# Two-network kernel: convolution taps without GpSimd, a re-ordered background preparation, and a new order of the first down tiles

## The chip, the cores and the metric

One core of a Trainium2 chip runs the whole program. The metric is device microseconds of one execution, the median of three runs. PE is TensorE, DVE is VectorE, ACT is ScalarE, POOL is GpSimd and SP is SyncE, whose queue issues the program's DMAs.

## The reference

A latent stream `x` and a context stream of 256 tokens each, 1024 wide, pass through two networks of two layers. Each layer is a half feed forward, a mixer, and another half feed forward. The three parts that the change touches compute:

```python
def _swiglu(h, wg, wu, wd):                       # each feed forward, D_FF = 2816
    return (jax.nn.silu(h @ wg) * (h @ wu)) @ wd

def _conv_module(h, w1, b1, wdw, bdw, lng, lnb, w2, b2):   # mixer of layer 0, first network
    a, gt = jnp.split(h @ w1 + b1, 2, axis=-1)
    u = a * jax.nn.sigmoid(gt)
    u = depthwise_conv(u, wdw, width=31) + bdw
    u = jax.nn.silu(_layernorm(u, lng, lnb))
    return u @ w2 + b2

def s5_discretise(lam_re, lam_im, b_re, b_im, log_step):   # mixer of layer 1, second network
    ...                                           # depends on weights alone
```

The S5 mixer's tables (powers of the diagonal, their products with B and C, a Toeplitz kernel) depend on weights alone, so they can be made at any time before the mixer.

## The kernel before, in words

Activations are kept transposed, features on partitions, in 8 tiles of 128. A matrix product in 32-bit precision is made of three matmuls (high x high, low x high, high x low) by `gemm`; `pump` splits each weight piece of 128x1024 into its high part (ACT, line 180) and low part (line 185, on DVE, or on GpSimd for every second piece when `cvm` is 2). Five pieces are held ready at most (`NBUF`), and `release` frees them and asks for the next.

**Feed forward** (`ffn`). The stages are named f100, f102, f110, f112 for the first network (layer, then 0 or 2 for the first or second half) and f200 to f212 for the second. The 22 hidden tiles are made in groups of 6, 8 and 8 (`FGROUPS`): for each hidden tile the products `gu` (gate and up), then `glu`: silu on ACT (`sg`, line 775), product on DVE (line 777), high part `Hh` on ACT (line 779), low part `Hl` on DVE (line 780). After a group come its 8 down tiles `pd`, each a sum over the group's hidden tiles (`down`), added to the stream by `scalar_tensor_tensor` or `tensor_add`. f112 and f212 have one stream of 256 columns, the others two (512 columns).

**Convolution** (`conv`, lines 947 to 1146). For each feature tile m the product `pw1` (48 matmuls) gives `u`. The 31 taps are shared out: 8 are scaled on ACT (line 998) and added up on GpSimd (line 999, tile `a`), 5 are matmuls with diagonal weights on PE (`ptap`), the other 18 run on DVE (line 1004) in two accumulators `v` and `b`; the sums meet in lines 1007, 1021 and 1022. The last tile has 7 on GpSimd and 12 on PE. `cvm` is 2 here. Then a layer norm (means by matmul, `pmean`) and `pw2`.

**S5 preparation** (`s5_pre`, lines 1853 to 2107) is a generator that runs as a `Task` beside f100, f102 and f110, with a period of 820 ns of the planner's PE time. A bare `yield` gives one period, `yield n` at least n ns. It makes 8 blocks d; in each, two directions r. For each r, GpSimd makes 6 wide products (`A8`, `B8`, lines 2015 to 2025), PE turns them (`pvt`), ACT copies them out, a DMA stores them (`dV`); then GpSimd makes 6 more (lines 2041 to 2051) in the same three tiles `w0` to `w2`, they are stored (`dO`), and PE multiplies them into `kp`. Then follow the rotations `E`, in the same tiles (lines 2079 to 2098), and the Toeplitz loads. What is left after f110 is drained at once.

The order on each engine's queue is made by the framework's scheduler from program order and its own estimate of when operands are ready. Each queue runs in order.

Of the kernel before, what the change touches and what calls it, by code (L numbers as in the profile page):

```python
# [7 lines left out]
F32 = mybir.dt.float32  # L8
F32R = mybir.dt.float32r
AF = mybir.ActivationFunctionType  # L10
# [4 lines left out]
KT = 8  # L15
# [3 lines left out]
NRAW = 3  # L19
LAT, CTX = 0, 1  # L20
# [448 lines left out]
class Net(Core):  # L469
# [245 lines left out]
    def ffn(self, b, streams, ready, gate, after, nsplit=4, first=1, work=None, side=None, head=0, tail=0, begin=None):  # L715
# [6 lines left out]
        with ExitStack() as es:  # L722
# [59 lines left out]
            def down(w, d, n6, c0, n, g, ss, start=None):  # L782
                start = d == 0 if start is None else start
                ps = self.psm.tile([128, 512], F32, tag="m", name="pd")
                rhs = lambda k: (Hh[k][:, c0:c0 + n], Hl[k][:, c0:c0 + n])
                self.gemm(ps[:, :n], w, rhs, [(k, k) for k in range(n6)])
# [16 lines left out]
            for g, (f0, nf) in enumerate(FGROUPS):  # L803
# [46 lines left out]
                if full < KT:  # L850
                    ws = {}
                    for s in streams:
                        ds = list(range(full, KT))
                        if tail and s != streams[0]:
                            ds = ds[2 * tail:] + ds[:2 * tail]
                        for d in ds:
                            if d not in ws:
                                ws[d] = self.take()
                            down(ws[d], d, nf, s * T, T, g, [s], full == 0 and d == ds[0])
                            if s == streams[-1] or d < 2 * tail:  # L860
                                self.release(1)
                                ws.pop(d)
# [84 lines left out]
    def conv(self, ready, gate, after, NPE=5, NPOOL=8, L=1, n1_=12, n2_=7):  # L947
# [3 lines left out]
        with self.pool("conv") as cp:  # L951
# [23 lines left out]
            def taps(m, ss, n_pe=NPE, n_pool=NPOOL):  # L975
# [4 lines left out]
                pk, ek, dk = range(n_pool), range(n_pool, n_pool + n_pe), list(range(n_pool + n_pe, W))  # L980
                a2 = cp.tile([128, 2, T], F32, tag="a2", name="a2", bufs=2)[:, :ns]
# [8 lines left out]
                def diagonal():  # L990
                    if len(dgs) < len(ek):
                        dg = cp.tile([128, 128], F32, tag="dgw", name="dgw", bufs=12)
                        nc.scalar.activation(out=dg, in_=self.ident, func=AF.Copy, scale=w(ek[len(dgs)]))
                        dgs.append(dg)
                for k in pk[1:]:
                    diagonal()
                    pr = cp.tile([128, 2, T], F32, tag="pr", name="pr", bufs=2)[:, :ns]
                    nc.scalar.activation(out=pr, in_=src(k), func=AF.Copy, scale=w(k))
                    nc.gpsimd.tensor_add(a2, a2, pr)
                while len(dgs) < len(ek):  # L1000
                    diagonal()
                for i, k in enumerate(dk[2:]):
                    o = (vm, b2)[i % 2]
                    ins = nc.vector.scalar_tensor_tensor(out=o, in0=src(k), scalar=w(k), in1=o, op0=ALU.mult, op1=ALU.add)
                    if i == 0:
                        first.append(ins)
# [7 lines left out]
                def rest():  # L1014
# [6 lines left out]
                    nc.vector.tensor_add(vm, vm, a2)  # L1021
# [69 lines left out]

            w0 = [self.take() for _ in range(2)]
# [15 lines left out]
            for s in S2:  # L1108
                for m in range(KT - L, KT):
# [16 lines left out]
                    taps(m, [s], *((n1_, n2_) if m == KT - 1 else ()))  # L1126
# [726 lines left out]
    def s5_pre(self, sp):  # L1853
# [40 lines left out]
        yield  # L1894
# [59 lines left out]
        def load(d):  # L1954
            bc = sp.tile([128, 4, 2, 4, 16], F32, tag="bc", name="bc")
# [4 lines left out]
        def toeplitz(d):  # L1960

            for hf in range(2):
                tt = sp.tile([128, 8, 72], F32, tag=f"w{hf}", name="tt")
                tt = tt.rearrange("p a b -> p (a b)")[:, :512].rearrange("p (g e) -> p g e", g=4)
# [6 lines left out]

        for d in range(8):
            bc = load(d)
# [4 lines left out]
            pw = [sp.tile([128, 2, 4, 9], F32, tag=f"pw{i}", name=f"pw{i}") for i in range(2)]  # L1978
            pt = [sp.tile([128, 8, 32], F32, tag=f"e{i}", name=f"pt{i}") for i in range(2)]
            v.memset(pn[0][:, :, 0:1], 1.0)  # L1980
# [4 lines left out]
            for k, n in ((1, 1), (2, 2), (4, 4)):  # L1985
# [3 lines left out]
                cmul(v, O[0], O[1], X[0], X[1], Y[0], Y[1], pt[0][:, :, :n], pt[1][:, :, :n])  # L1989
# [11 lines left out]
            yield 6000  # L2001
# [5 lines left out]
            for r in (1, 0):  # L2007

                k0 = r
                pr, pi = [w[:, r, :, k0:k0 + 8].unsqueeze(3).to_broadcast([128, 4, 8, 16]) for w in pw]  # L2010
                br, bi = [b[:, r].unsqueeze(2).to_broadcast([128, 4, 8, 16]) for b in bb]
                A, B, C = [sp.tile([128, 4, 9, 16], F32, tag=f"w{i}", name=f"w{i}") for i in range(3)]
                A8, B8, C8 = [t.rearrange("p q e h -> p (q e h)")[:, :512].rearrange("p (q e h) -> p q e h", q=4, e=8)
                              for t in (A, B, C)]
                g.tensor_mul(A8, pr, br)
                yield
                g.tensor_mul(C8, pi, bi)
                yield
                g.tensor_add(A8, A8, C8)
                yield  # L2020
                g.tensor_mul(B8, pr, bi)
                yield
                g.tensor_mul(C8, pi, br)
                yield
                g.tensor_sub(B8, B8, C8)
                yield 6000
                for i, s_ in enumerate((A8, B8)):
# [4 lines left out]
                    vt = (C8, A8)[i].rearrange("p q e h -> p (q e h)")  # L2032
                    a.activation(out=vt, in_=ps, func=AF.Copy)
                    yield 2500
                    nc.sync.dma_start(out=self.dV[d][r][:, i * 512:i * 512 + 512], in_=vt)
                    yield 3000
# [3 lines left out]
                A, B, C = [sp.tile([128, 4, 9, 16], F32, tag=f"w{i}", name=f"w{i}") for i in range(3)]  # L2040
# [11 lines left out]
                yield 6000  # L2052
                k0 = 1 - r
                for i, s_ in enumerate((A, B)):
# [3 lines left out]

                kp = self.psa.tile([128, 512], F32, tag="a", name="kp")
                fl = lambda t, q, x, y: t[:, q, x:y, :].rearrange("p e h -> p (e h)")  # L2060
# [13 lines left out]
                yield 3000  # L2074
            nc.sync.dma_start(out=self.dK[d], in_=kt)

            E = [sp.tile([128, 8, 72], F32, tag=f"w{i}", name=f"E{i}") for i in range(2)]
            E = [e.rearrange("p a b -> p (a b)")[:, :512].rearrange("p (a b) -> p a b", a=8) for e in E]
            g.memset(E[0][:, :, 0:1], 1.0)
            g.memset(E[1][:, :, 0:1], 0.0)  # L2080
            for i, t in enumerate((c8, s8)):
                g.tensor_copy(E[i].rearrange("p (d q) e -> p d q e", d=2)[:, :, :, 1], col(t))
            yield
            k = 1
            while k < 63:
                n = min(k, 63 - k)
                X = [p[:, :, 1:1 + n] for p in E]
# [6 lines left out]
                if n > 4:  # L2094
                    yield
# [378 lines left out]
```

## Time and profile before

| | us |
|---|---|
| median of 3 runs (lowest to highest) | 3753.76 (3747.49 to 3756.62) |
| the profiled execution | 3753.8 |
| its span, first to last instruction | 3752.0 |
| PE busy | 3495.2 (93%) |
| DVE busy | 2652.6 (71%) |
| ACT busy | 1424.2 (38%) |
| GpSimd busy | 1218.5 (32%) |
| mean granted TensorE clock | 0.963 |

The outer 1.8 us lie outside the span. Busy shares are averages over stages of different kinds; PE's busy time also holds stretches at the lower of its two clocks. The stages in the trace: f100 from 29 us, convolution from 446 us, f102 from 716 us, f110 from 1095 us, the attention of the first network from 1508 us, f112 from 1726 us to 1939 us, then the second network.

### The profile page before, as it was taken

The page shows a single profiled execution, that of the slowest core. Times are in us where ns is not written, and L with a number is a line of the kernel's source. Part 1 is how long each engine was busy: PE and PEld are TensorE (multiplying, and loading weights), DVE is VectorE, ACT ScalarE, POOL GpSimd, SP SyncE. Part 2 cuts the span into 40 slices and gives each one's busy share as a digit, 9 for nine tenths or more (in the row PEclk, how much of TensorE's full clock was granted, in tenths as well). Part 3 has the DMA queues.
Part 4 walks back from the last instruction along what each step waited for, and adds up shares of the span by engine and source line. Part 5 has one row for each costly group of instructions (what it writes and reads, how often), then busy time and mean ns, then how long its engine had stood idle before and what let it go on. Part 6 is the DMA issues. An engine that isn't in the chain of part 4 may idle for free. (4 is left out here: it accounts for less than half of the span.)

```text
span 3752.0 us, 54881 instructions
## 1 busy us (share of the span) xinstructions
PE 3495.2 (93%) x21110; PEld 3055.5 (81%) x21110; DVE 2652.6 (71%) x4326; ACT 1424.2 (38%) x2500; POOL 1218.5 (32%) x1057
## 2 busy tenths in 40 slices
PE   8989977999999899998999998999999999997898
PEld 7767855988898687898998888778888988885798
DVE  7988699776669786777987775786665633368633
ACT  4222344532233223555343223565322432243443
POOL 5545366244445355213430003333000300035343
PEclk9999988999999999999999999999999999998899
DMA  7565310254546863424655542103555332238353
GB/s 258 184 207 194 118 57 34 102 192 164 167 146 211 293 211 130 144 89 160 244 217 199 185 165 96 62 29 107 180 192 178 135 124 92 100 114 281 113 191 125
DMA packets 158127, 580.42 MB, mean 155 GB/s; under 512 B 25252, under 2 KB 56740, under 8 KB 118184
## 3 DMA queue, kind: packets, MB, share of 16 engines
q1 hardware_dynamic: 157864, 576.91, 44.4%
q8 instruction: 166, 2.72, 0.3%
q14 instruction: 97, 0.79, 0.1%
HBM read 547.55 MB, written 29.29 MB: 154 GB/s over the span
## 5 line engine op out<-in xcount | busy, mean ns | idle before, releaser
L180 ACT ACTIVATE wh<-raw 128x1024 fp32r<-128x1024 f32 (+1 forms) x679 | 701.2, 1038 | 1268.4 <-PE gu L106 728.5
L106 PE MATMUL gu<-hl,wh 128*128 128x512 f32 (+1 forms) x3136 | 1084.6, 347 | 5.4 <-DVE hl L693 4.4
L106 PE MATMUL gu<-hh,wh 128*128 128x512 f32 (+1 forms) x3136 | 1078.9, 348 | 8.4 <-ACT hh L690 7.8
L106 PE MATMUL gu<-hh,wl 128*128 128x512 f32 (+1 forms) x3136 | 1083.2, 347 | 2.8 <-DVE wl L185 2.5
L185 DVE TENSOR_TENSOR wl<-raw,wh 128x1024 fp32r<-128x1024 f32 (+1 forms) x537 | 694.1, 1295 | 401.2 <-ACT wh L180 389.8
L185 POOL TENSOR_TENSOR wl<-raw,wh 128x1024 fp32r<-128x1024 f32 (+1 forms) x142 | 360.1, 2537 | 1259.4 <-ACT wh L180 1214.7
L535 DVE CUSTOM_DVE_ANT_0 jk<-mw,cb,vec 128x1024 bf16<-128x1024 f32 x480 | 705.8, 1470 | 29.7 <-DMA mw<-in_mw_dram 19.0
L106 PEld LDWEIGHTS gu<-hl,wh 128*128 128x128 f32 x3136 | 600.5, 192 | 79.1 <-DVE hl L693 6.1
L106 PEld LDWEIGHTS gu<-hh,wh 128*128 128x128 f32 x3136 | 597.0, 192 | 81.7 <-ACT hh L690 9.4
L106 PEld LDWEIGHTS gu<-hh,wl 128*128 128x128 f32 x3136 | 600.2, 192 | 74.3 <-DVE wl L185 3.5
L106 PE MATMUL pd<-Hh,wh 128*128 128x256 f32 (+1 forms) x1696 | 562.7, 334 | 27.4 <-ACT Hh L779 27.3
L106 PE MATMUL pd<-Hl,wh 128*128 128x256 f32 (+1 forms) x1696 | 563.6, 334 | 1.6 <-DVE Hl L780 1.5
L106 PE MATMUL pd<-Hh,wl 128*128 128x256 f32 (+1 forms) x1696 | 563.5, 334 | 0.0
L106 PEld LDWEIGHTS pd<-Hh,wh 128*128 128x128 f32 x1696 | 323.9, 192 | 60.3 <-ACT Hh L779 29.3
L106 PEld LDWEIGHTS pd<-Hl,wh 128*128 128x128 f32 x1696 | 324.5, 192 | 33.5 <-DVE Hl L780 2.8
L106 PEld LDWEIGHTS pd<-Hh,wl 128*128 128x128 f32 x1696 | 324.5, 192 | 30.3 <-issue 0.2
L777 DVE TENSOR_TENSOR gu<-sg,gu 128x512 f32<-128x512 f32 (+1 forms) x196 | 113.2, 578 | 205.5 <-PE gu L106 196.0
L106 PE MATMUL pj<-hh,wh 128*128 128x256 f32 (+1 forms) x736 | 230.4, 330 | 16.9 <-ACT hh L690 6.9
L106 PE MATMUL pj<-hh,wl 128*128 128x256 f32 (+1 forms) x736 | 232.3, 320 | 0.9 <-DVE wl L185 0.9
L106 PE MATMUL pj<-hl,wh 128*128 128x256 f32 (+1 forms) x736 | 231.1, 319 | 1.7 <-DVE hl L1086 1.0
L779 ACT ACTIVATE Hh<-gu 128x512 fp32r<-128x512 f32 (+1 forms) x196 | 98.7, 503 | 287.6 <-DVE gu L777 287.6
L106 PEld LDWEIGHTS pj<-hh,wh 128*128 128x128 f32 x736 | 145.5, 206 | 28.9 <-ACT hh L690 8.2
(407 smaller groups left out, 4656.3 us busy)
## 6 DMA issues: line engine op xcount, KB each, us to landing
raw<-in_gu_dram SPq DMA_DIRECT2D x186, 1024.0 KB, 4.8
mw<-in_mw_dram SPq DMA_DIRECT2D x280, 512.0 KB, 4.2
raw<-in_dn2b_dram SPq DMA_DIRECT2D x38, 1024.0 KB, 4.7
raw<-in_dn1b_dram SPq DMA_DIRECT2D x32, 1024.0 KB, 6.2
raw<-in_dn1a_dram SPq DMA_DIRECT2D x16, 768.0 KB, 4.3
raw<-in_pw_dram SPq DMA_DIRECT2D x12, 1024.0 KB, 4.7
raw<-in_dn2a_dram SPq DMA_DIRECT2D x16, 768.0 KB, 4.2
dV<-w SPq DMA_DIRECT2D x32, 256.0 KB, 4.2
```

Of the source, the lines that this page charges most:

```text
L106: ins = self.last_mm = self.nc.tensor.matmul(out=out, lhsT=lhsT, rhs=rhs, start=start, stop=stop, **kw)
L180: ins = nc.scalar.activation(out=h2, in_=r, func=AF.Copy)
L185: self.low_p = lambda eng=eng, l2=l2, r=r, h2=h2: eng.tensor_sub(l2, r, h2.bitcast(F32))
L535: self.behind_pe(nc.vector.tensor_tensor_reduce(out=jk, in0=tl[i], in1=self.cb[s], scale=1.0, scalar=self.V(f"mod_b{b}{l}")[:, j:j + 1], o ...
L777: nc.vector.tensor_mul(pr[:, :n], sg[:, :n], pu[:, :n])
L779: nc.scalar.activation(out=hi, in_=pr[:, :n], func=AF.Copy)
```

## The change

Four edits:

- In `conv` no tap runs on GpSimd any more: 8 taps on PE, 23 on ACT and DVE (the first two of them as ACT's initial values of `v` and `b`). The last tile has 14 on PE. `cvm` is 0 until the context stream's layer norm, so the weights' low parts are made on DVE.
- In `s5_pre` the pieces of a block become functions, called in another order: inputs(1), outputs(1), turned(1), inputs(0), stores, steps(1), outputs(0), turned(0), rotations, stores, steps(0). Inputs, outputs, turned tiles and small temporaries have tiles of their own, the block's table is loaded one block ahead, the copies into `bbz` move from ACT to GpSimd, most long yields go, and the period is 1500.
- In `ffn` the down tiles 0 and 1 of a group (three tiles for the first stream of a last group that is worked stream by stream) run together: all hidden tiles but the last for each, then the last hidden tile for each.
- `dynamic_dma_scratch_size` is set to 1024.

```diff
+PRE_STEP = 1500
...
-            def down(w, d, n6, c0, n, g, ss, start=None):
...
+            def downs(items, n6, c0, n, g, ss, start):
+
+                pss = [self.psm.tile([128, 512], F32, tag="m", name="pd") for _ in items]
                 rhs = lambda k: (Hh[k][:, c0:c0 + n], Hl[k][:, c0:c0 + n])
-                self.gemm(ps[:, :n], w, rhs, [(k, k) for k in range(n6)])
+                for (w, d), ps in zip(items, pss):
+                    self.gemm(ps[:, :n], w, rhs, [(k, k) for k in range(n6 - 1)], True, False)
+                for (w, d), ps in zip(items, pss):
+                    self.gemm(ps[:, :n], w, rhs, [(n6 - 1, n6 - 1)], False, True)
+                    added(ps, d, c0, g, ss, d == start)
...
-                for d in range(full):
-                    w = self.take()
-                    down(w, d, nf, 0, N, g, streams)
-                    self.release(1)
+                d = 0
+                while d < full:
+                    m = 2 if d == 0 else 1
+                    downs([(self.take(), d + i) for i in range(m)], nf, 0, N, g, streams, 0)
+                    self.release(m)
+                    d += m
...
-    def conv(self, ready, gate, after, NPE=5, NPOOL=8, L=1, n1_=12, n2_=7):
+    def conv(self, ready, gate, after, NPE=8, L=1, n_last=14):
...
-                first = [nc.vector.tensor_scalar(b2, src(dk[1]), w(dk[1]), None, ALU.mult)]
-                nc.scalar.activation(out=a2, in_=src(0), func=AF.Copy, scale=w(0))
+                nc.scalar.activation(out=b2, in_=src(dk[1]), func=AF.Copy, scale=w(dk[1]))
...
-                for k in pk[1:]:
-                    diagonal()
-                    pr = cp.tile([128, 2, T], F32, tag="pr", name="pr", bufs=2)[:, :ns]
-                    nc.scalar.activation(out=pr, in_=src(k), func=AF.Copy, scale=w(k))
-                    nc.gpsimd.tensor_add(a2, a2, pr)
...
-                    nc.vector.tensor_add(vm, vm, a2)
                     nc.vector.tensor_add(vm, vm, pe)
...
+            self.cvm = 0
             w0 = [self.take() for _ in range(2)]
...
             self.cv_behind = None
+            self.cvm = 2
             mean(KT - 1, CTX)
...
-            bc = load(d)
+            bc = ahead
+            if d < 7:
+                ahead = load(d + 1)
...
-                a.activation(out=bbz[i][0:64, :, :, 0:16], in_=bb[i][0:64], func=AF.Copy)
-                a.activation(out=bbz[i][64:128, :, :, 16:32], in_=bb[i][64:128], func=AF.Copy)
+                g.tensor_copy(bbz[i][0:64, :, :, 0:16], bb[i][0:64])
+                g.tensor_copy(bbz[i][64:128, :, :, 16:32], bb[i][64:128])
...
+            V1 = yield from inputs(1)
+            O1 = yield from outputs(1)
+            yield from turned(1, V1)
+            V0 = yield from inputs(0, lambda: store_outputs(1, O1))
+            yield from steps(1, O1)
+            O0 = yield from outputs(0)
+            yield from turned(0, V0)
+            E = yield from rotations()
+            store_outputs(0, O0)
+            yield from steps(0, O0)
+            store_rotations(E)
             nc.sync.dma_start(out=self.dK[d], in_=kt)
...
+            yield 4000
             yield from toeplitz(d)
...
-            pre = Task(self, self.s5_pre(sp), 820)
+            pre = Task(self, self.s5_pre(sp), PRE_STEP)
...
-    nc = _bacc.Bacc("TRN2", target_bir_lowering=False, num_devices=1)
+    nc = _bacc.Bacc("TRN2", target_bir_lowering=False, num_devices=1, dynamic_dma_scratch_size=1024)
```

The new functions are the old bodies: `inputs` and `outputs` hold 6 wide GpSimd operations and 6 yields each, `turned` eight matmuls, two ACT copies and two stores with four yields (two of them of 1500), `steps` 16 matmuls and the two sums into `kt` (yields of 2000 and one period), `rotations` 36 small GpSimd operations with 10 yields.

## Rows read from the trace of the kernel before

**Rows 1.** Waits of PE, whole span: who for whom, us in total, times, longest

```profile
PE pmean L106 <- DVE v L1022: 27.7, 5, 10.0
PE pd L106 <- ACT Hh L779: 27.3, 6, 14.8
...
PE kp L106 <- POOL w L2051: 14.0, 5, 4.8
...
PE kp L106 <- POOL w L2045: 10.0, 4, 5.1
...
PE pvt L106 <- POOL w L2019: 4.5, 1, 4.5
```

**Rows 2.** Windows: us, busy us (instructions) PE PEld DVE ACT POOL, PEclk, DMA, GB/s

```profile
2692.70:2779.90 87.20, 87.20 (x386) 72.23 (x385) 50.49 (x68) 25.44 (x34) 0.00 (x0) 1.00 0.50 176
472.00:647.40 175.40, 129.76 (x485) 93.20 (x483) 173.57 (x184) 84.83 (x161) 113.83 (x69) 0.84 0.12 42
142.80:239.60 96.80, 91.64 (x430) 74.18 (x429) 86.86 (x133) 24.16 (x34) 59.77 (x58) 1.00 0.62 204
239.40:301.90 62.50, 47.62 (x218) 38.20 (x217) 54.39 (x73) 14.07 (x20) 30.47 (x22) 0.89 0.63 212
824.90:915.50 90.60, 90.60 (x434) 74.21 (x433) 56.53 (x65) 27.41 (x38) 43.90 (x52) 1.00 0.49 171
915.50:959.00 43.50, 43.50 (x194) 36.02 (x193) 29.98 (x66) 10.27 (x14) 18.57 (x22) 1.00 0.50 161
1207.50:1315.10 107.60, 94.17 (x410) 76.54 (x409) 81.47 (x131) 28.26 (x41) 46.40 (x42) 0.92 0.79 272
1360.40:1460.80 100.40, 92.27 (x414) 75.34 (x413) 69.44 (x110) 27.12 (x40) 44.09 (x48) 0.95 0.51 174
```

**Rows 3.** Groups by form of the convolution, 446 to 716 us, VectorE and GpSimd

```profile
L1004 DVE SCALAR_TENSOR_TENSOR v<-u,vec,v 128x512 f32<-128x512 f32 x56 | 69.7, 1251 | 0.0
...
L969 DVE SCALAR_TENSOR_TENSOR u<-th,t 128x256 f32<-128x256 f32 x16 | 7.5, 482 | 0.0
...
L999 POOL TENSOR_TENSOR a<-a,pr 128x512 f32<-128x512 f32 x49 | 86.3, 1762 | 55.0 <-ACT pr L998 52.3
```

**Rows 4.** Timeline of VectorE in the convolution: start us, us

```profile
516.28 1.41 DVE L1004 SCALAR_TENSOR_TENSOR v<-u,vec,v 128x512 f32<-128x512 f32 x2
517.60 1.41 DVE L1004 SCALAR_TENSOR_TENSOR b<-u,vec,b 128x512 f32<-128x512 f32 x2
...
560.73 1.21 DVE L185 TENSOR_TENSOR wl<-raw,wh 128x1024 fp32r<-128x1024 f32 x1
...
568.18 1.77 DVE L1004 SCALAR_TENSOR_TENSOR v<-u,vec,v 128x512 f32<-128x512 f32 x1
```

**Rows 5.** Timeline of PE in the convolution

```profile
474.51 4.46 PE L106 MATMUL ptap<-u,dgw 128*128 128x512 f32 x10
...
612.78 7.57 PE L106 MATMUL ptap<-u,dgw 128*128 128x512 f32 x10 [3.48 <-DVE u L969]
...
620.90 1.03 PE L106 MATMUL pmean<-v,invm 128*128 128x256 f32 x4
```

**Rows 6.** Timeline of the longest stall of PE, 249 to 262 us

```profile
250.85 0.31 ACT L2003 ACTIVATE bbz<-bb 64x128 f32<-64x128 f32 x1 [9.23 <-POOL bb L1949]
...
260.66 0.80 PE L106 MATMUL pd<-Hh,wh 128*128 128x512 f32 x1 [14.79 <-ACT Hh L779]
```

**Rows 7.** Timeline of PE at two group ends of the one-stream feed forward f112

```profile
1835.51 0.38 PE L106 MATMUL pd<-Hh,wh 128*128 128x256 f32 x1 [2.68 <-ACT Hh L779]
...
1841.81 0.80 PE L106 MATMUL pd<-Hh,wh 128*128 128x256 f32 x2 [2.61 <-ACT Hh L779]
...
1915.28 0.38 PE L106 MATMUL pd<-Hh,wh 128*128 128x256 f32 x1 [2.29 <-ACT Hh L779]
```

**Rows 8.** Line 1956 (the S5 tables' loads): durations, first and last start

```profile
L1956 SPq DMA_DIRECT2D bc<-in_s5bc_dram x8: 347/433/1135, 87.8 to 1386.8; - x8
```

**Rows 9.** Groups of GpSimd, whole span

```profile
L2045 POOL TENSOR_TENSOR w<-w,w 128x576 f32<-128x576 f32 x16 | 34.2, 2135 | 1.3
```

More of the change, by code (lines that the diff above doesn't have):

```diff
@@ L855, in ffn @@
                             ds = ds[2 * tail:] + ds[:2 * tail]
[L856 to L862, printed above, removed]
+                        start = ds[0] if full == 0 else None
+                        while ds:
+                            m = 3 if full == 0 and s == streams[0] and len(ds) == KT else 1
+                            now, ds = ds[:m], ds[m:]
+                            for d in now:
+                                if d not in ws:
+                                    ws[d] = self.take()
+                            downs([(ws[d], d) for d in now], nf, s * T, T, g, [s], start)
+                            for d in now:
+                                if s == streams[-1] or d < 2 * tail:
+                                    self.release(1)
+                                    ws.pop(d)
                         after(s, acc[s])
@@ L1977, in s5_pre @@
             pn = [sp.tile([128, 8, 9], F32, tag=f"pn{i}", name=f"pn{i}") for i in range(2)]
-            pw = [sp.tile([128, 2, 4, 9], F32, tag=f"pw{i}", name=f"pw{i}") for i in range(2)]
+            pw = [sp.tile([128, 2, 4, 9], F32, tag=f"pw{i}", name=f"pw{i}", bufs=2) for i in range(2)]
             pt = [sp.tile([128, 8, 32], F32, tag=f"e{i}", name=f"pt{i}") for i in range(2)]
+            pv = [sp.tile([128, 8, 4], F32, tag=f"pq{i}", name=f"pq{i}") for i in range(2)]
             v.memset(pn[0][:, :, 0:1], 1.0)
@@ L2101, in s5_pre, with rotations @@
-            yield 5000
-            for r in range(2):
-                for i, t in enumerate(E):
-                    nc.sync.dma_start(out=self.dE[d][r][:, i * 256:i * 256 + 256],
-                                      in_=t[:, 4 * r:4 * r + 4, :].rearrange("p q e -> p (q e)"))
-                yield
+                yield
+            def rotations():
+                E = [sp.tile([128, 8, 64], F32, tag=f"vw{i}", name=f"E{i}") for i in range(2)]
+                g.memset(E[0][:, :, 0:1], 1.0)
+                g.memset(E[1][:, :, 0:1], 0.0)
+                for i, t in enumerate((c8, s8)):
+                    g.tensor_copy(E[i].rearrange("p (d q) e -> p d q e", d=2)[:, :, :, 1], col(t))
+                yield
+                k = 1
+                while k < 63:
+                    n = min(k, 63 - k)
+                    X = [p[:, :, 1:1 + n] for p in E]
+                    Y = [p[:, :, k:k + 1].to_broadcast([128, 8, n]) for p in E]
+                    O = [p[:, :, k + 1:k + 1 + n] for p in E]
+                    t1, t2 = pt[0][:, :, :n], pt[1][:, :, :n]
+                    g.tensor_mul(t1, X[0], Y[0])
+                    g.tensor_mul(t2, X[1], Y[1])
+                    g.tensor_sub(O[0], t1, t2)
+                    if n > 4:
+                        yield
+                    g.tensor_mul(t1, X[0], Y[1])
+                    g.tensor_mul(t2, X[1], Y[0])
+                    g.tensor_add(O[1], t1, t2)
+                    k += n
+                    yield
+                return E
@@ new lines, in store_rotations @@
+            def store_rotations(E):
+                for r in range(2):
+                    for i, t in enumerate(E):
+                        nc.sync.dma_start(out=self.dE[d][r][:, i * 256:i * 256 + 256],
+                                          in_=t[:, 4 * r:4 * r + 4, :].rearrange("p q e -> p (q e)"))
+            V1 = yield from inputs(1)
[3 more added lines that the diff above has]
+            yield from steps(1, O1)
```

110 lines of the change are left out of this document (45 added, 65 removed).

## The prediction

> **What bounds the kernel now.** I read the page first: PE is busy 93% of the span, so what counts is where PE waits and where its granted clock is low. The waits of PE come next. Three things stand out there [rows 1]: the convolution's means wait for DVE (27.7 us), down tiles wait for `Hh` from ACT (27.3 us, one wait alone 14.8), and the S5 preparation's matmuls wait for GpSimd (`kp` and `pvt`, 28.5 us in the rows shown). Then I cut the span into stretches [rows 2]. The reader is to see two things. First, a stretch of 8 hidden tiles without background work takes 87.2 us, which is 0.227 us for each of its 384 matmuls; beside the preparation it takes 90.6 us in f102, but 96.8, 107.6 and 100.4 us in f100 and f110. Eight down tiles take 43.5 us in f102 and 62.5 us in f100. Wherever the excess is large, so is the idle time, and the clock is below 1.00 behind it. Second, from 472 to 647 us in the convolution DVE is busy for 173.6 of 175.4 us and PE for 129.8: DVE sets the pace there.
>
> **Convolution, DVE.** The same pass over 128x512 (line 1004) has two prices in the timeline. With GpSimd idle two passes take 1.41 us and the next one starts 1.32 us after them, so 0.66 us each; while GpSimd adds, one takes 1.77 us [rows 4]. Their mean was 1.25 us, and 49 GpSimd adds of 1.76 us lie among them [rows 3]. The change takes away all of these adds. A tile m now costs DVE 21 passes and two sums (lines 1007 and 1022, taken at the price of a pass), 23 x 0.66 = 15.2 us; two pieces' low parts at 1.2 us [rows 4], where one was GpSimd's, 2.4 us; and two `u` of 0.48 [rows 3], 1.0 us. That is 18.6 us.
>
> The Trainium skill (Perfetto Trace Analysis, Optimizing Scalar/DVE Operations) says that work of a saturated DVE may go to ScalarE or even GpSimd, and that offloading to GpSimd might not help, since the two share an SBUF read port. By the first half, three more passes a tile would cost 7 x 3 x 0.66 = 14 us instead of gaining, and the time would be 3718 us; the trace bears out the second half, with 1.77 against 0.66 us.
>
> **Convolution, PE.** A tile costs 48 matmuls x 0.227 = 10.9 us; 8 taps where 5 took 4.46 us, so 7.1 us; and two means a stream pair, 1.0 us [rows 2, 5]. That is 19.0 us at the higher clock, above DVE's 18.6. Five taps at a partly lower clock took 7.57 us [rows 5]. The tiles' taps started at 474.51 and, six tiles on, at 612.78 [rows 5]: 23.0 us a tile before. If both engines pack without a gap, the six steps save 6 x 4.0 = 24 us, and the last tile, which no longer waits for GpSimd's sum `a` nor for DVE's backlog, saves up to 15 more: 39 us is the lower end. No gain at all is excluded only if the slow passes are GpSimd's doing; the upper end is the rival below. Between them I take 30, near the packed end, because the quick price stands in the same tile as the slow one and PE has a whole tile of slack before a mean needs its `v`. ACT loses 8 scalings a tile and gains 3 diagonals and a scaling; it is not near its limit (84.8 of 175.4 us [rows 2]) and costs nothing while that holds.
>
> **Preparation.** The longest stall shows the mechanism [rows 6]: ACT's copy into `bbz` waits 9.23 us for GpSimd, which waits for the block's table; silu of the last hidden tile is queued behind it on ACT, and PE then stands for 14.79 us and comes back at the lower clock, 1.2 of 2.4 GHz (granted 0.89 in that stretch [rows 2]). The change loads the table a block ahead and puts the copies on GpSimd, so nothing of ACT is behind them. The other waits, `kp` and `pvt` for GpSimd, come since a product's six operations were followed by 6000 ns of lag at most. The widest of them takes 2.14 us on average [rows 9], so six can take 12.8 us. In the new order twelve steps of 1.5 us lie between the first of `inputs` and `turned`: 18 us; and `steps` comes 10 or more steps behind the last of its `outputs`. So the products are ready although GpSimd may need up to 24 x 2.14 = 51 us for what 24 steps schedule in 36; the rotations and the Toeplitz yields let it catch up. Own tiles also remove GpSimd's waits on the stores.
>
> The price: four stretches compared with f102, which holds the same matmuls and the same preparation without a wait [rows 2]: 96.8 - 90.6 = 6.2, 62.5 - 43.5 = 19.0, 107.6 - 90.6 = 17.0, 100.4 - 90.6 = 9.8, together 52.0 us, low clock included. I take 48; the lower end is 60, as the shorter stretches of the two stages hold a few more us; the upper end is 8 (a rival). DMAs: the same stores and loads are issued, each on SP's queue behind work that is further ahead, so the weight loads behind them wait less; I cost that at nothing, and a longer wait would be covered by the three loads in flight. The pace: a block's yields summed to 118 us of planner time (23 long ones, 88 us, and 37 of 0.82) and now sum to 104 (8 long ones, 29 us, and 50 of 1.5). Eight loads of the table lie between 87.8 and 1386.8 us [rows 8]; less the convolution and the down tiles without background, some 137 us a block. So the new block needs some 120 us, and eight still end about with f110. What is left is drained there, as the last block was before.
>
> **Down tiles.** The f100 wait of 14.79 us and one of the same kind are counted above, since their cause is the `bbz` copy. What remains is f112: PE waited 2.68, 2.61 and 2.29 us there [rows 7]. But the first and the third of these are 18 matmuls after the start, six hidden tiles: there the seventh, not the last, is late, and the new order still needs it at the same place. Only the second, for the last, gains. DVE is the late one in f112, so a later wait takes some of it back. On the other side two weight pieces are released together, after the second tile; three ready ones cover that for three tiles. Costs from -6 (all of the waits but the first) to +5 (two waits for low parts of 2.5 us at the ends of groups, as long as the longest wait above); I take -2. The scratch size moves no instruction: 0.
>
> **Sum.** 3753.8 - 30 - 48 - 2 = 3673.8 us, against the profiled execution, which equals the median of the runs. Ends: 3753.8 - 39 - 60 - 6 = 3649 and, without a rival, 3753.8 - 20 - 38 + 5 = 3701.
>
> **Rivals.**
> (a) PE becomes the bound of the convolution and waits remain at the tile ends, so that the 23.0 us go down to 21.5 only: 10 us gained, 3694 us. For it: 19.0 and 18.6 us are nearly equal, and each engine's delay then reaches the other. Against it: three `u` buffers and a tile of slack. Chance 0.12.
> (b) The preparation's stalls come back in another place: GpSimd gets 51 us of work in 36 us, and each of the 8 blocks makes PE wait once for 5 us (the longest `kp` wait, [rows 1]), 40 us: 3714 us. For it: GpSimd is shared with a busy DVE in f100 and f110. Against it: the lags above. Chance 0.12.
> (c) Slower: PE's clock stays low through the convolution. Granted clock is 0.84 there now [rows 2]. At half rate a tile costs PE 2 x 19.0 = 38 us, 15 more than before; seven tiles cost 105 us, and the time is 3753.8 + 105 - 48 - 2 = 3809. It decides from 50/15, some 3.3 low tiles of seven. Against it: in the tiles without a long wait the taps ran at the high clock (4.46 us), and 3 more taps fill the gaps. Chance 0.04. The Trainium skill (TensorE: Matmul & The Clock Gate, HAM oscillation) describes such a loop, which falls back to the lower clock in every round because it waits in every round; here the waits shrink, and no row shows which side wins.
> (d) The slow DVE passes are not GpSimd's doing: 23 x 1.25 + 3.4 = 32 us a tile, 9 more in seven tiles, 63 us: 3767 us. Two prices that change with GpSimd's adds speak against it. Chance 0.02.
> (e) The change doesn't do what it says: the scheduler, which orders by its own estimate, puts the matmuls back where they waited, and the gains of one part pay for the other's losses; no change. Chance 0.04.
>
> **How the numbers follow.** The forecast, all three parts about as summed, has 0.66. Rivals (a) and (b) are faster too: 0.90 in all; (e) is 0.04 within 0.3%, which is about what a measurement of this kernel can tell from no change (11 us); (c) and (d) are 0.06 slower. The range reaches from a little below the lower end to past (b): 3640 to 3718 us; the forecast's own is 3649 to 3701.
>
> **What would show it.** Right: no GpSimd work between 472 us and the layer norm, all 128x512 passes at 0.66 to 0.75 us, the taps of successive tiles about 19 to 20 us apart, granted clock near 1.00, DVE no longer at 99%; `kp` and `pvt` waits of PE below 5 us in total; hidden-tile stretches of f100 and f110 at 91 to 93 us; no ACT wait for `bb`. f112 about as long as before. Wrong: tiles more than 22 us apart, a clock still near 0.84 in the convolution, or PE waiting for GpSimd in every block.

## The result and the profile after

The changed kernel takes 3690.11 us in the median (3685.34 to 3694.68), against 3750.62 for the kernel before on the same chip: a ratio of 0.9831 (0.9818 to 0.9844), 60 us less. Forecast were 3674 us, 80 us below the 3753.8 that the sum starts from, in a range from 3640 to 3718. The total hides two errors of opposite sign. By the trace the convolution lost 39 us where 30 were forecast, and the preparation's stretches gained far less than 48.

The stages in us, each read from its first matmul to the first of the next; f100 and f110 end with their last `pd` matmul, and the convolution's count starts there:

| | before | after | difference | forecast |
|---|---|---|---|---|
| f100 | 416.9 | 409.0 | -7.9 | about -23 |
| convolution | 269.8 | 230.5 | -39.3 | -30 |
| f102 | 379.2 | 380.7 | +1.5 | 0 |
| f110 | 412.6 | 401.7 | -10.9 | about -25 |
| f112 | 212.7 | 210.6 | -2.1 | -2 |

The rest of the span moved by under 2 us. The forecast for f100 and f110 shares the 48 us out by their two excess stretches each (25.2 and 26.8 of 52.0).

Windows of the changed kernel, with the columns of [rows 2]: the two long stretches of f100, the convolution, an undisturbed down stretch of f102, and the first, third, fourth and fifth stretches of f110.

```profile
142.20:238.20 96.00, 92.79 (x433) 75.11 (x431) 95.76 (x165) 23.17 (x34) 86.41 (x78) 0.98 0.57 186
239.90:302.30 62.40, 49.82 (x201) 39.76 (x202) 57.08 (x79) 12.22 (x15) 23.30 (x12) 0.89 0.64 223
468.00:608.00 140.00, 135.32 (x542) 95.21 (x541) 137.02 (x216) 54.86 (x116) 5.30 (x4) 0.99 0.13 46
868.20:913.70 45.50, 45.50 (x218) 37.34 (x217) 30.65 (x45) 10.40 (x13) 13.25 (x9) 1.00 0.44 157
1049.70:1135.90 86.20, 75.14 (x517) 69.20 (x516) 73.56 (x113) 30.56 (x55) 57.22 (x65) 0.94 0.61 201
1169.20:1259.00 89.80, 89.80 (x426) 73.65 (x425) 78.06 (x98) 21.94 (x31) 73.09 (x69) 1.00 0.81 281
1258.80:1317.30 58.50, 51.22 (x222) 40.36 (x221) 51.62 (x68) 15.83 (x20) 20.14 (x13) 0.91 0.67 235
1317.30:1405.80 88.50, 88.50 (x406) 72.94 (x405) 64.12 (x95) 25.31 (x34) 32.93 (x46) 1.00 0.57 196
```

The reader is to see four things. The convolution now has both engines full, PE 135 and DVE 137 of 140 us, at a clock of 0.99 (0.84 before, [rows 2]). The two eight-tile hidden stretches of f110 went from 107.6 and 100.4 to 89.8 and 88.5 us, as forecast. But f100's pair stands where it stood, 96.0 and 62.4, and f110 has two new excesses: 86.2 us in its first stretch (77.1 before) and 58.5 in a down stretch (45.3 before). In f100's 96.0 us DVE is busy for 95.8, where it was busy for 86.9 of 96.8 before.

Waits of PE over the whole span:

```profile
PE pd L107 <- ACT Hh L780: 17.5, 7, 4.9
PE pd L107 <- DVE Hl L781: 11.3, 8, 3.3
PE pvt L107 <- POOL vw L2026: 8.1, 1, 8.1
PE pmean L107 <- DVE v L1025: 3.5, 2, 1.8
PE pvt L107 <- POOL vw L2034: 2.7, 1, 2.7
```

`pmean` fell from 27.7 to 3.5 us, `kp` is gone, and the single wait of 14.8 us for `Hh` with it [rows 1]. What came instead is spread: fifteen waits of the down tiles for `Hh` and `Hl`, 28.8 us, in sum as much as their nine before (27.3 and 1.5 us), and one of 8.1 us for GpSimd.

The timeline shows the three places. First f100's second down stretch (PE), and DVE and GpSimd ahead of it:

```profile
243.48 2.43 DVE L536 CUSTOM_DVE_ANT_0 jk<-mw,cb,vec 128x1024 bf16<-128x1024 f32 x1
...
247.84 0.69 DVE L778 TENSOR_TENSOR gu<-sg,gu 128x512 f32<-128x512 f32 x1
```

```profile
242.43 2.40 POOL L2063 TENSOR_TENSOR ow<-ow,ow 128x576 f32<-128x576 f32 x1
244.79 2.04 POOL L2024 TENSOR_TENSOR vw<-pw,bb 128x512 f32<-128x512 f32 x1
```

```profile
249.21 0.54 PE L107 MATMUL pd<-Hh,wh 128*128 128x512 f32 x1 [4.94 <-ACT Hh L780]
253.03 0.79 PE L107 MATMUL pd<-Hl,wh 128*128 128x512 f32 x1 [3.28 <-DVE Hl L781]
```

A modulation pass (line 536, a product of a 128x1024 weight row with the broadcast conditioning row, summed) takes 2.43 us beside GpSimd's products. The hidden tile's product (line 778) stands behind such passes on DVE, and PE stands behind it. ACT, which the waits name, had itself waited 9.6 us for line 778. Then f110's second down stretch, with ACT ahead of PE, and the transposes in its first stretch:

```profile
1264.27 1.06 ACT L507 ACTIVATE cb<-cb 128x1024 f32<-128x1024 f32 x1 [8.41 <-DMA cb<-in_c_dram]
```

```profile
1266.81 0.80 PE L107 MATMUL pd<-Hh,wh 128*128 128x512 f32 x1 [3.78 <-ACT Hh L780]
```

```profile
1111.30 0.90 PE L107 MATMUL pvt<-cst,vw 128*128 128x128 f32 x3 [8.06 <-POOL vw L2026]
```

At 1264 us ACT had stood 8.41 us at the SiLU of the second network's conditioning row (`cb`), which was still being loaded; the last hidden tiles' SiLU was behind it.

**Theory and rivals.** My theory after this reading was that each stretch has its own cause: in f100 DVE, slowed by GpSimd; in f110's down stretch ACT's wait for `cb`; at 1111 us the order of GpSimd's queue. The rivals: that the parts of the change hinder each other (each alone would gain what was forecast), that the new order of the down tiles makes the waits, and that the preparation's density alone explains all three.

### The profile page after: what moved, and what is told of

Same layout as the page of the kernel before. It is cut to its first block, busy times and chain, and to the rows that moved or that the text cites. A ratio compares the mean times of both kernels' runs of the same rounds, so it can differ in the third digit from the quotient of the medians.

```text
span 3691.4 us, 54762 instructions
## 1 busy us (share of the span) xinstructions
PE 3497.5 (95%) x21160; PEld 3058.1 (83%) x21160; DVE 2641.6 (72%) x4360; ACT 1380.8 (37%) x2430; POOL 1199.6 (32%) x1021
## 5 line engine op out<-in xcount | busy, mean ns | idle before, releaser
L186 DVE TENSOR_TENSOR wl<-raw,wh 128x1024 fp32r<-128x1024 f32 (+1 forms) x544 | 706.8, 1302 | 367.7 <-ACT wh L181 360.1
L186 POOL TENSOR_TENSOR wl<-raw,wh 128x1024 fp32r<-128x1024 f32 (+1 forms) x135 | 344.3, 2553 | 1278.4 <-ACT wh L181 1216.3
```

Source lines behind the costliest of these rows:

```text
L186: self.low_p = lambda eng=eng, l2=l2, r=r, h2=h2: eng.tensor_sub(l2, r, h2.bitcast(F32))
```

## The experiments

Ratios are to the kernel before on the same chip, with 95% intervals. For stretches the profiled execution of each run is read.

**The three parts alone.** The kernel before with the hunks of one part each; the scratch size goes with the preparation.

```diff
-    def conv(self, ready, gate, after, NPE=5, NPOOL=8, L=1, n1_=12, n2_=7):
+    def conv(self, ready, gate, after, NPE=8, L=1, n_last=14):
```

> The kernel before with the convolution's edit alone (no GpSimd taps, 8 taps on TensorE instead of 5, weight low parts on VectorE there). Theory (each part is worth what its stretches of the trace lost): 39 us faster than before, within 5, all of it between the start of the convolution and the start of the next feed forward, 270 to about 230 us; no tap product or sum on GpSimd, VectorE's passes 0.75 us. Rival (the parts depend on each other: with the old preparation the 39 us is partly the preparation's): 30 us or less, with the missing 9 us in the convolution's stretch. Second rival: the stages behind it shift in phase against the old preparation and lose or win more than 8 us there.

Measured: 0.9884 (0.9870 to 0.9899), 44 us less. The convolution went from 269.8 to 230.3 us, f100 from 416.9 to 412.5, and the stages behind it stayed within 1 us. So the convolution's gain is its own: DVE busy 136.42 and PE 135.31 of 140 us, as in the changed kernel.

```diff
-            pre = Task(self, self.s5_pre(sp), 820)
+            pre = Task(self, self.s5_pre(sp), PRE_STEP)
```

> The kernel before with the preparation's edit alone (lagged steps, own buffers, period 1500, smaller descriptor scratch). Theory: 19 us faster, within 6: the waits of PE for kp and for its bbz chain go, but about 30 us re-form as waits of the group ends for the hidden tiles. Rival: the preparation by itself is worth the 48 us that was forecast, and only the new phases against the changed convolution and down tiles bring the waits back: 40 us or more faster. Second rival: 8 us or less, since without the down pairs the late last hidden tiles cost more.

Measured: 0.9961 (0.9946 to 0.9976), 15 us less. f100 took 416.8 us (416.9 before), f110 400.2 (412.6), f112 209.5 (212.7). So none of the 8 us by which f100 got shorter in the changed kernel is the preparation's. The same stretches as in the changed kernel are long: 63.9 us for f100's second down stretch and 58.2 for f110's, and the transposes wait 5.6 us. So they come from the preparation's edit itself, not from its meeting with the others; that rival falls.

```diff
-            def down(w, d, n6, c0, n, g, ss, start=None):
+            def downs(items, n6, c0, n, g, ss, start):
```

> The kernel before with the down tiles' edit alone (first two together with the last input tile at the end, three in the one-stream feed forward). Theory: 2 us faster, within 5, all of it where the first down tile waited for its last hidden tile (up to 2.7 us in each of six group ends). Rival: 13 us or more faster, the one-matmul waits being longer in sum than the rows of the waits gave. Second rival: slower by over 5 us, as two accumulators are held open and the hidden tiles of the next group wait for a free bank.

Measured: 0.9983 (0.9974 to 0.9993), 7 us less. The profiled execution was the slowest of its ten, so its stretches don't show where. The three ratios together make 1.7%, the change made 1.7%: the parts add.

**The old order of the down tiles in the changed kernel.**

> The changed kernel with the old order of the down tiles. Theory: the pair covers part of the late last hidden tile in the groups where that tile is late (14 us of waits in the second group of the first feed forward, 7 us in that of the third), so without it the kernel is 5 to 15 us slower than the changed one, that is 3696 to 3705 us, with the difference in these two groups. Rival: the pair only moves the wait to its second half and covers nothing: within 3 us of the changed kernel. Second rival: the pair makes the waits (its first half needs the seventh hidden tile at once): 5 us or more faster than the changed one.

Measured: 3693.38 us, 0.9834 (0.9818 to 0.9851), no difference from the changed kernel's 0.9831 that its intervals tell. In the profiled executions f100's second down stretch took 64.7 instead of 62.3 us and f110's 61.1 instead of 58.5. These two executions lie 10 us apart and their runs' medians don't, so that the pair covers 2.5 us of a late last tile isn't shown; that it doesn't make the waits is.

**No preparation beside f100.** `side=pre` is left out of the call of f100. The preparation runs from f102 on, its rest alone behind f110.

> The changed kernel with no preparation beside the first feed forward (f100); the preparation starts in f102 and what is left of it after f110 runs alone, so only f100's stretches are read, not the time. Theory (VectorE is the bound of f100's second group, and its 1.28 us modulation passes take up to 2.4 us because GpSimd works beside them): the passes of f100 take 1.28 to 1.35 us in the mean (1.53 to 1.67 in its second group now), the second down stretch takes 44 to 48 us instead of 62.4, and the six-tile stretch before it 88 to 90 instead of 96. Rival (the modulation's 1 us of broadcast load and accumulate slows itself, or VectorE has too much to do in any case): the passes stay over 1.5 us, or the down stretch stays over 58 us.

First line 536 in f100, duration minimum, median and maximum in ns, then the two stretches of f100:

```profile
L536 DVE CUSTOM_DVE_ANT_0 jk<-mw,cb,vec x112: 1271/1278/1286, 66.8 to 363.9; 128x1024 bf16<-128x1024 f32 x112
```

```profile
141.90:228.90 87.00, 87.00 (x385) 72.03 (x385) 70.25 (x100) 24.77 (x31) 0.00 (x0) 1.00 0.56 198
228.90:272.40 43.50, 43.50 (x194) 36.02 (x193) 36.35 (x60) 8.94 (x9) 0.00 (x0) 1.00 0.55 194
```

The same line in the changed kernel:

```profile
L536 DVE CUSTOM_DVE_ANT_0 jk<-mw,cb,vec x112: 1267/1284/2511, 66.8 to 395.4; 128x1024 bf16<-128x1024 f32 x112
```

All 112 passes take 1.27 to 1.29 us when GpSimd is silent; beside it some take up to 2.51. DVE has 70 of 87 us to do instead of 96 of 96, PE never waits, and f100 as a whole takes 376.3 us, 33 less. (The kernel is slower, 3734.6 us in its one execution, as the preparation's rest runs alone behind f110.) The preparation's own matmuls account for 4 to 5 us of the 30 us in these two stretches (89.8 us where a hidden stretch with the preparation had no wait, and 45.5 such a down stretch), and a wait of the transposes for GpSimd for 2.7; the rest is VectorE's delay and the low clock that follows it.

GpSimd's products aren't all that is missing here. The preparation also has small operations of its own on DVE, the powers of a block's tables (`pn`). Windows of f100's hidden stretch with these alone (busy us of DVE and POOL, then the last three columns of [rows 2]), before and after the change:

```profile
142.80:239.60 96.80, 3.48 (x26) 0.00 (x0) 1.00 0.62 204
142.20:238.20 96.00, 22.34 (x71) 0.00 (x0) 0.98 0.57 186
```

One and the same operation in the changed kernel, first beside GpSimd's wide products, then with GpSimd idle:

```profile
149.79 1.02 DVE L1953 TENSOR_TENSOR pq<-pn 128x8 f32<-128x8 f32 x1
186.70 0.16 DVE L1953 TENSOR_TENSOR pq<-pn 128x8 f32<-128x8 f32 x1
```

The edit brought the powers of nearly three blocks into this stretch, where one block's had been, and beside the products they take up to 1.4 us each. The passes take 51.1 us there for 31, against 42.2 us for 33 without the preparation. So DVE is full for two reasons, slower passes and the preparation's own work on it. The run takes both away together; how the 33 us divide between them is not shown.

**Fewer modulation passes at a time.** In f100 their period is stretched by 12% after the first group.

```diff
+                if g == 0 and task is not None:
+                    task.period *= slow
```

> The changed kernel with the modulation passes of f100 paced 12% slower after its first group (they end at 395 us now, and are needed from about 420 us on). Theory (VectorE's queue overflows in the second group: 96 of 96 us busy, then 59 of 64): with fewer passes there the last hidden tiles come earlier, the 14 us of waits in the second down stretch shrink by half or more, and the kernel is 5 to 12 us faster than the changed one. Rival (the burst of GpSimd's products at 225 to 253 us alone makes the tiles late, whatever the pace): 0 to 3 us. Second rival: the passes that are left over delay the last group, and the kernel is slower.

Measured: 0.9821 (0.9808 to 0.9835), 3684.7 us. The down stretch went from 62.3 to 55.7 us, the hidden one (here up to the first down matmul) from 97.7 to 94.9, f100 from 409.0 to 401.3. So taking work off DVE shortens it, though waits of 3.8 and 3.0 us are left there; the whole gain, 4 us by the ratios, is within the intervals.

**ACT's SiLU of the conditioning rows, later.** The loads stay where they are, the SiLU is issued 20 us of planner time later; in the second run it is also tied to the matmul before it.

```diff
-            self.nc.scalar.activation(out=t, in_=t, func=AF.Silu)
...
+    def silu_c(self):
+        for t in self.cb:
+            self.behind_pe(self.nc.scalar.activation(out=t, in_=t, func=AF.Silu))
```

> The changed kernel, where in the third feed forward (f110) ScalarE's SiLU of the two broadcast conditioning rows is issued 20 us of modelled TensorE work after their loads instead of right behind them. Theory (the 58.7 us of this stage's second down stretch are 46 us of work and a wait of ScalarE, whose queue stands 8.4 us at that SiLU with the last hidden tiles' SiLU behind it): the stretch takes 45 to 49 us, the kernel gets 8 to 12 us faster than the changed one, 3678 to 3682 us. Rival (the hidden tiles are late because VectorE is behind there, with the modulation passes and GpSimd's preparation; ScalarE's wait only coincides): stretch and time stay within 3 us.

> As the run with the later SiLU of the broadcast rows, but with that SiLU also ordered behind the matmul at whose issue the 20 us are over; without this order the scheduler had put it back to its old place, and ScalarE still waited 6.8 us. Theory (ScalarE's wait is what makes the last hidden tiles of this group late): the wait of ScalarE goes, the second down stretch of f110 takes 45 to 48 us (58.5 changed, 53.0 with the later issue alone), and the kernel is 9 to 13 us faster than the changed one, about 3679 us. Rival (VectorE's modulation passes then come late and take its place): the stretch stays at 52 us or more, or the hidden stretch behind it gets 4 us longer.

Issued later alone: 0.9817 (0.9803 to 0.9830), the down stretch 53.0 us. But ACT's row had hardly moved:

```profile
1262.97 1.06 ACT L511 ACTIVATE cb<-cb 128x1024 f32<-128x1024 f32 x1 [6.83 <-DMA cb<-in_c_dram]
```

The scheduler had put it back in front of the hidden tiles. With the tie: 0.9786 (0.9772 to 0.9800), 3677.81 us, 17 us better by the ratios than the changed kernel, and the stretch is as short as an undisturbed one:

```profile
1261.00:1306.80 45.80, 45.80 (x222) 37.56 (x221) 43.38 (x57) 15.10 (x19) 20.86 (x13) 1.00 0.68 245
```

So ACT's wait was the cause there, all 12.7 us of it: 7.3 us of PE's waits, and the rest at the lower clock that followed (granted 0.91 in the changed kernel, 1.00 here). The preparation is as dense as before, so its density isn't the cause of this one. The kernel before had nearly the same wait of ACT (its waits from 1207 to 1361 us), but inside the eight-tile hidden stretch, where PE had matmuls left:

```profile
ACT cb L506 <- DMA cb<-in_c_dram: 7.0, 1, 7.0
```

The edit didn't make this wait; by shortening the stage it moved the wait to the end of a group, where PE has nothing else. Counted from the start of f110, the row was ready after 209.7 us before and 214.5 after, while the first down matmul behind this hidden stretch came forward from 219.7 to 209.1.

**The transposes at 1111 us.** First GpSimd's order is held as issued (outputs behind inputs), then the rotations get 3 us a step.

```diff
-                g.tensor_mul(A, pr, cr)
+                self.behind(g.tensor_mul(A, pr, cr), last[0])
```

> The changed kernel, where the first product of each block's outputs is held in GpSimd's queue behind the last operation of its inputs, the order in which the text of the kernel issues them. Theory (the scheduler put outputs ahead of inputs, so that TensorE's transposes stood 8.1 us at 1111 us for GpSimd's tile, and 2.7 us at 154 us): these waits go, the first hidden stretch of f110 takes 76 to 80 us instead of 86.4, and the kernel is 8 to 11 us faster than the changed one. Rival (the lag is only moved: the output products are then late for the products of the steps, or GpSimd's backlog meets the next transposes): kp waits of 3 us or more come back and less than 4 us are gained.

Measured: 0.9835 (0.9821 to 0.9848), no gain, and the wait grew:

```profile
1106.68 1.11 PE L107 MATMUL pvt<-cst,vw 128*128 128x128 f32 x4 [13.90 <-POOL vw L2028]
```

The tile itself came sooner, 56.2 us after the start of f110 instead of 61.6. But in PE's queue the transposes now stood behind 314 recorded `gu` matmuls of f110 instead of 384, and so asked for it earlier still. The order inside GpSimd's queue is thus worth some 5 us for the tile, but alone it doesn't set the wait: that depends as much on where the scheduler puts the transposes, and there my theory failed. The `kp` waits of the rival didn't come either. The edit ties only the first of the six products of the outputs; another one, of 2.2 us, still ran ahead of the inputs.

```diff
-                    yield
+                    yield 3000
```

> The changed kernel with 3 us instead of 1.5 us between the steps of a block's rotations, some 15 us more a block. Theory (GpSimd has fallen behind the plan there: it works without a gap from 1062 to 1110 us, its rotations take 27 us where 15 are planned, and the transposes behind them come 8.1 us too early for it): the waits for GpSimd's tile at 154 and 1111 us go, f110's first hidden stretch takes 77 to 80 us instead of 86.2, and the kernel is 6 to 10 us faster than the changed one. Rival (the wait follows from where the preparation stops at the end of f102 and starts again, not from the pace): the wait stays or moves to another block, and what is gained is under 3 us. Second rival: the preparation no longer ends inside f110, and its rest, drained alone, makes the kernel slower.

Measured: 0.9817 (0.9800 to 0.9834), 3689.2 us; the 5 us by the ratios are within the intervals. The wait at 1111 us went and f110's first stretch took 77.1 us, as forecast (the wait at 154 us stayed, 2.8 us); then the next one took 45.4 instead of 33.3. The rows of that stretch, PE, then the waits of DVE and of SP's queue ahead of it (us in total, times, longest):

```profile
1143.24 1.22 PE L107 MATMUL pd<-Hh,wh 128*128 128x512 f32 x2 [9.99 <-ACT Hh L780]
```

```profile
DVE jk L536 <- DMA mw<-in_mw_dram: 11.7, 2, 9.0
```

```profile
SPq L2129 <- POOL E L2116: 14.5, 1, 14.5
```

SP's queue stood 14.5 us at the store of the rotations, which GpSimd hadn't finished. The modulation weights were queued behind it; DVE waited 9.0 us for them, then did the missed passes with one more wait of 2.75 us, and the last hidden tile stood behind these. So the time came out as the rival said, but not for its reason: the pace did remove the wait at 1111 us. GpSimd's lag reappeared one queue further.

**One tap less on PE.** `NPE=7`.

> The changed kernel with 7 instead of 8 of the convolution's 31 taps on TensorE, so one pass more a tile on VectorE. Read from the convolution's stretch (229.5 to 230.8 us in all kernels with the new convolution). Theory (both engines are at their bound, TensorE busy 135 and VectorE 137 of 140 us, so a tap less on the one makes the other the bound): one pass of 0.745 us more a tile, 233 to 236 us, and TensorE gets gaps. Rival (TensorE alone is the bound, and VectorE's passes only look full): a tap of 0.89 us less a tile, 224 to 227 us.

Measured in the convolution's stretch, in one execution: 237.1 us. The window over the same 140 us, and PE at the ends of the last tiles:

```profile
468.00:608.00 140.00, 128.35 (x514) 90.92 (x512) 137.00 (x219) 50.88 (x108) 1.41 (x2) 0.94 0.13 46
```

```profile
592.99 2.08 PE L107 MATMUL pmean<-v,invm 128*128 128x256 f32 x4 [3.28 <-DVE v L1025]
601.07 1.22 PE L107 MATMUL pmean<-v,invm 128*128 128x256 f32 x2 [6.00 <-DVE v L1025]
```

6.6 us more, a little over the forecast, as DVE's backlog is paid at the end. The rival, TensorE alone as the bound, falls. With 8 taps the two engines are about level (135 and 137 of 140 us); 9 taps were not run.

**Three cures together.** The tied SiLU, the slower passes, and `yield 9000` ahead of the seventh block's first transposes.

> The changed kernel with three things together: the SiLU of the broadcast rows issued later and held there (alone 12 us), the modulation passes of f100 12% slower after the first group (alone 5 us), and 9 us more before the transposes in the one block (the seventh) whose transposes waited 8.1 us. Theory (three stalls with three causes, each in its own stretch): they add, 3690 - 12 - 5 - 8 = 3665 us, at most 3670, with f100 at 402, f110's first hidden stretch at 77 to 79 and its second down stretch at 46 us. Rival (as in the run with slower rotations, VectorE's modulation passes or SyncE's queue put another wait in the place of the one at 1111 us): 3672 to 3677 us, with a wait of 6 us or more in f110's first two stretches.

Measured: 3668.77 us, 0.9761 (0.9747 to 0.9774), 88 us below the kernel before and the fastest of all. f100 took 400.8 us and f110's second down stretch 45.3, as expected. The third cure failed, and the wait that was the rival's sign is there:

```profile
1101.72 0.90 PE L107 MATMUL pvt<-cst,vw 128*128 128x128 f32 x3 [8.07 <-POOL vw L2036]
```

The transposes still stood behind the same 384 recorded `gu` matmuls of f110 as in the changed kernel, although 9 us had been put ahead of them. That agrees with a scheduler that puts them back, as it did with the SiLU; transposes tied to the matmul before them were not run. That the time still met the theory's "at most 3670" is in part luck: f100 gave 8.2 us where 5 were counted, the down stretch 13.2 for 12, and the convolution and f102, which no cure touches, came out 2 us shorter.

## Why the prediction was right and wrong

**Convolution: the mechanism right, the term 9 us too small.** Groups and timeline of the changed kernel:

```profile
L1008 DVE SCALAR_TENSOR_TENSOR v<-u,vec,v 128x512 f32<-128x512 f32 x77 | 55.3, 745 | 2.6 <-ACT v L997 2.6
```

```profile
513.97 1.41 DVE L1008 SCALAR_TENSOR_TENSOR b<-u,vec,b 128x512 f32<-128x512 f32 x2
515.29 1.41 DVE L1008 SCALAR_TENSOR_TENSOR v<-u,vec,v 128x512 f32<-128x512 f32 x2
```

```profile
505.08 7.04 PE L107 MATMUL ptap<-u,dgw 128*128 128x512 f32 x16
523.76 7.04 PE L107 MATMUL ptap<-u,dgw 128*128 128x512 f32 x16
```

Two passes start every 1.32 us, 0.66 each, as costed; the 0.745 us of the group is the duration with the overlap of neighbours. Eight taps take 7.04 us (costed 7.1), and the tiles in the middle are 18.68 us apart (costed 19.0). So the working led to its lower end of 39 us. Its two parts came out otherwise: from the first tile's taps to the seventh's it is 106.0 us instead of 138.3, so the six steps saved 32 where 24 were costed, and the last tile and the rest 7 where up to 15 were. That the sum is 39 is in part luck. The step that failed is the choice of 30, "near the packed end": the allowance for gaps between two nearly equal engines, which was rival (a). There are none in these tiles. Rivals (c) and (d) are out by the clock of 0.99 and the 0.66 us.

**Preparation: 48 us forecast, some 15 measured alone (interval 9 to 20).** What was said of the waits held in part: `kp` went, ACT no longer waits for `bb`, the hidden stretches of f110 take 89.8 and 88.5 us; but PE's waits at `pvt` came to 10.8 us, where `kp` and `pvt` together were to stay below 5. The step that failed is the price, "four stretches compared with f102 ... without a wait". It put the whole excess of f100 and f110 down to the preparation's waits on PE. Two things in it were other. In f100 the bound is DVE, with 112 modulation passes in the stage, slowed by GpSimd's work beside them, and with the preparation's own operations. The stretches compared weren't alike in that, and [rows 2] showed it: DVE was busy for 86.9 of 96.8 us in f100 and for 56.5 of 90.6 in f102. The edit undid ACT's stall but filled that queue further (95.8 of 96.0 us in the hidden stretch; in the down stretch 57.1 of 62.4, 54.4 of 62.5 before), and the same stretch was only lost to another name. In f110 the gain of 30 us in two stretches is there, but 9 us at the transposes and 13 us at ACT's wait for `cb` came instead. That is rival (b) in its sense, stalls that re-form, though not in its form: not one GpSimd wait in each of 8 blocks but three places, and only one of them a wait named for GpSimd. In size, too, 15 us lie nearer to the rival's 8 than to 48. "The products are ready although GpSimd may need up to 51 us" failed at that one: GpSimd still was 8 us late.

That the total lies between the forecast's own ends is in part luck. With the convolution's 30 and the other two parts as measured alone it would have been 3753.8 - 30 - 15 - 7 = 3702 us, past the upper end of 3701; and for the 20 and 38 us in that end the working gives no rows.

The Trainium skill (SBUF — State Buffer, SBUF: two separate sides) says that DVE and GpSimd share a port pair as a lock: the one that starts first keeps it for its whole instruction, and the other waits. By that rule a pass and a product that alternate would each take about the sum of both, 2.34 us by an estimate from the shortest times here (1.28 us for a pass, 1.06 for a 128x512 product). The traces agree roughly: beside each other passes took up to 2.5 us and the product 2.0 in the median. The small operation above agrees too: with 0.16 us of its own it took 1.02 beside a product.

**Down tiles: -2 forecast, -7 (-10 to -3) alone, nothing that can be told in the changed kernel.** The 2.1 us by which f112 got shorter in the table look like the forecast but can't be put down to the pair: f112 took 209.5 us with the preparation alone and the old order, 211.5 in the changed kernel with the old order, and 207.7 to 211.2 in the other kernels with the new one. As forecast the seventh hidden tile is the late one in f112: PE still waits for it there.

```profile
1780.33 0.38 PE L107 MATMUL pd<-Hh,wh 128*128 128x256 f32 x1 [2.69 <-ACT Hh L780]
```

The scratch size was not run alone. The preparation ended sooner than costed, with its last store at 1375.5 us, some 76 us before the end of f110, and nothing was drained after it.

## What to carry over

Before a stretch's excess is put down to the wait that the trace names, look whether another engine is full in it: here VectorE's busy time (96 of 96 us) told more than the releaser, and the stage without the preparation was 33 us shorter. When background work is made denser, look at what it costs on every engine that it uses: here it had 22 us of small operations on the fullest one. A wait that lies hidden inside a stage costs nothing until the stage is shortened around it; follow every long wait of the side engines, not only PE's, to where it will fall next. When a scheduler orders queues by its own estimate, an instruction issued later is not later in the queue until it is tied there: the same edit gave 53.0 us untied and 45.8 tied.

## What was not expected of the hardware

The contention between VectorE and GpSimd works both ways and nearly at full price. VectorE's 1.28 us pass takes up to 2.51 us, its 0.16 us operation up to 1.4 (1.02 in the row shown), and one and the same product of GpSimd in the changed kernel (minimum, median and maximum in ns) takes 1.06 or 2.0:

```profile
L2024 POOL TENSOR_TENSOR vw<-pw,bb x16: 1061/2003/2143, 139.9 to 1245.6; 128x512 f32<-128x512 f32 x16
```

With slower rotations the store of one late tile held SyncE's whole queue for 14.5 us, and reached TensorE through VectorE and ScalarE as a wait of 10 us with ScalarE's name on it.
